# First stage of a transformer layer: modulation pair by pair, and transposes placed behind their copies

## The chip, the cores and the metric

The kernel runs on one core of a Trainium2 chip. The metric is the device time of one execution in microseconds (us). Three runs of the kernel before took 2655.70, 2655.83 and 2657.45 us, median 2655.83 us. The profiled execution took 2657.01 us; its span in the trace is 2655.3 us, so 1.71 us lie around the span.

## The reference

One layer of a hybrid backbone works on 256 latent tokens x and 256 context tokens ctx, both 2048 wide, all in fp32. What this case touches is its beginning:

```python
mod_x = (jax.nn.silu(c) @ w_mod[i] + b_mod[i]).reshape(bsz, 1, N_MOD, D_MODEL)
mod_c = (jax.nn.silu(c_ctx) @ w_mod[i] + b_mod[i]).reshape(1, 1, N_MOD, D_MODEL)

def _half_ffn(x, mod, k, g, w_gate, w_up, w_down):
    h = _modulate(_rms_norm(x, g), mod[:, :, 3 * k], mod[:, :, 3 * k + 1])
    f = (jax.nn.silu(h @ w_gate) * (h @ w_up)) @ w_down
    return x + 0.5 * mod[:, :, 3 * k + 2] * f
```

`_modulate(h, shift, scale)` is `h * (1 + scale) + shift`. The nine modulation vectors come from one matrix `w_mod` of 2048 x 18432, and parts 0 (shift) and 1 (scale) of it must be there before any row of h exists. The feed-forward has 5504 hidden columns. A token mixer, a second half feed-forward and a final norm follow; the change leaves them alone.

## The kernel before

All activations stand transposed: 16 tiles of 128 features by 512 tokens (256 latent, 256 context), taken two at a time as eight *K pairs*, kp 0 to 7. Each fp32 operand of a large matmul is split into a rounded high part and the rest, low: ScalarE casts the high part (L68), VectorE subtracts (L69), and one product becomes three matmuls (`mm3`, L116 to L118). The cast and the subtraction of a weight tile together are called its *split* below.

The first stage, the first 150 us, does three things at once. It transposes x and ctx and sums their squares for the norm. It computes parts 1 and 0 of the modulation on TensorE (L529): the weights arrive in loads of 512 KB, a *half* is the work on two loads, four halves fill one PSUM *bank* of 512 columns, VectorE copies the bank to SBUF (L373, the *copy*), TensorE transposes it in four pieces (L378, the *turn*), and VectorE reduces the pieces to columns, adds the bias and scales (L381, L386, L393). With `cnt == 2` the two parts have a bank each, and a bank serves two K pairs; the loads have rows of 2 KB. With `cnt == 1` one bank holds both parts of a single K pair, and the loads have rows of 1 KB. The turn and its columns let `first_h` run for the K pair: VectorE multiplies by the norm (L324), ScalarE applies scale and shift (L332, tiles hh), VectorE makes the low part (L337, tiles hl). Third, `first_cols` multiplies hh and hl of each K pair with the first 384 columns of the gate and up weights of the first feed-forward, 18 matmuls for gate and 18 for up per K pair; these add up in six PSUM banks over all eight K pairs.

The order is written by hand: the lists given to `weave` say behind which group of three matmuls ("place", twelve a K pair) each half, copy and turn stands. K pairs 0 and 1 have their modulation complete before the first such matmul. `run` hands out the load and the split of a task two tasks ahead, and `ahead` keeps three halves' loads in front. A scheduler may then move instructions on an engine, but TensorE's modulation matmuls and VectorE's copies are marked with `keep_in_program_order`. Each engine works through its own queue in order.

All these weights pass through one pool of seven buffers (`rp`, tiles raw), loaded from SyncE's queue in order; a load is issued when the last reader of its buffer is done. After this stage the kernel streams the rest of the weights with TensorE as the busy engine.

Of the kernel before, what the change touches and what calls it, by code (L numbers as in the profile page):

```python
# [34 lines left out]
def tile_block(ctx: ExitStack, tc: tile.TileContext, a, out: bass.AP):  # L35
# [280 lines left out]
    def modulated(kp, vs, R, G, S):  # L316

        st = {}
        a0, a1 = vs[0] * TX, (vs[-1] + 1) * TX

        def scale():
            for v in vs:
                st[v] = slot([P, 2, TX], n="xr")
                tt(st[v], xpair(kp, v), R(v).unsqueeze(1).broadcast_to([P, 2, TX]), op=ALU.mult)  # L324

        def affine():
            for i in range(2):
                k = 2 * kp + i
                t = st["t", i] = slot([P, a1 - a0], n="t")
                for dst in (hh[k][:, a0:a1], t):  # L330
                    for v in vs:
                        act(dst[:, v * TX - a0:(v + 1) * TX - a0], st[v][:, i, :], AF.Identity, scale=G(k, v), bias=S(k, v))  # L332

        def parts():
            for i in range(2):
                k = 2 * kp + i
                tt(hl[k][:, a0:a1], st["t", i], hh[k][:, a0:a1].bitcast(F32), op=ALU.subtract)  # L337

        return [(0.7, scale), (0.1, affine), (0.8 * len(vs), parts)]
# [56 lines left out]
    def column(part):  # L396
        return lambda k, v: MOD[part][:, k, v:v + 1]
# [153 lines left out]
    def first_h(kp):  # L551
        for _, f in modulated(kp, (0, 1), lambda v: R0["R"][:, v * TX:(v + 1) * TX], column(1), column(0)):
            f()

    m0, t0 = first_mods(0, 2)
    for load, _ in m0:
        if load:
            load()
    total, root, spread = [f for _, f in pieces]
    for f in (*[f for _, f in m0[:5]], total, small_turn, root, *[f for _, f in m0[5:7]], t0[0], spread,  # L560
              *[f for _, f in m0[7:]], *t0[1:], lambda: first_h(0)):
        f()

    between = {1: [lambda: first_h(1)]}
    later = []

    def place(at, f):
        between.setdefault(at, []).append(f)  # L570

    def weave(k0, cnt, at):
        steps, turns = first_mods(k0, cnt)
        for (load, f), x in zip(steps, at):
            if load:
                later.append(load)
            place(x, f)
            if load:
                place(x, ahead)
        place(at[len(steps)], lambda: [t() for t in turns])  # L580
        place(at[len(steps)], lambda: first_h(k0))
        if cnt == 2:
            place(12 * k0 + 1, lambda: first_h(k0 + 1))
# [2 lines left out]
        if later:  # L586
            later.pop(0)()

    weave(2, 2, [1, 3, 5, 7, 8, 9, 11, 13, 15, 16, 17])
    weave(4, 2, [19, 21, 24, 26, 27, 29, 32, 34, 37, 38, 39])  # L590
    weave(6, 1, [42, 46, 50, 54, 55, 56])
    weave(7, 1, [58, 62, 66, 70, 71, 73])

    g0 = []

# [106 lines left out]
    for ci, n in enumerate(chunks):  # L702
        m0 = m
# [707 lines left out]
    t0 = len(tasks) - 8  # L1411
# [108 lines left out]
```

## Time and profile before

| what | value |
|---|---|
| median of three runs | 2655.83 us |
| the profiled execution, its span | 2657.01 us, 2655.3 us |
| TensorE busy in the span | 2616.2 us (99%) |
| VectorE, ScalarE busy | 1617.7 us (61%), 979.6 us (37%) |
| first matmul of the feed-forward | at 49.03 us |

The page gives the busy time of each engine, then slices of the span, then the chain of work that ended last. Such shares are means over the whole span; the stretch of the change, from 18 to 150 us, is read in the timeline, instruction by instruction: which engine a wait of TensorE is put down to, and what that engine had been waiting for in its turn. A row of the timeline may stand for several instructions of one form (x8), and its bracket gives the idle time before it and what ended that.

### The profile page before, as it was taken

The page shows a single profiled execution, that of the slowest core. Times are in us where ns is not written, and L with a number is a line of the kernel's source. Part 1 is how long each engine was busy: PE and PEld are TensorE (multiplying, and loading weights), DVE is VectorE, ACT ScalarE, POOL GpSimd, SP SyncE. Part 2 cuts the span into 40 slices and gives each one's busy share as a digit, 9 for nine tenths or more (in the row PEclk, how much of TensorE's full clock was granted, in tenths as well). Part 3 has the DMA queues.
Part 4 walks back from the last instruction along what each step waited for, and adds up shares of the span by engine and source line. Part 5 has one row for each costly group of instructions (what it writes and reads, how often), then busy time and mean ns, then how long its engine had stood idle before and what let it go on. Part 6 is the DMA issues. An engine that isn't in the chain of part 4 may idle for free.

```text
span 2655.3 us, 31810 instructions
## 1 busy us (share of the span) xinstructions
PE 2616.2 (99%) x12309; PEld 2132.3 (80%) x12309; DVE 1617.7 (61%) x2167; ACT 979.6 (37%) x1326; POOL 56.2 (2%) x84
## 2 busy tenths in 40 slices
PE   6999999999999999999999999999999999999998
PEld 3577888888888888888889977778788888888896
DVE  3378987876555556556324855876654445455646
ACT  4342222212222222222223654765564443434344
POOL 2000000000000000000000000021010000000000
PEclk8999999999999999999999999999999999999999
DMA  9976766657665766766434543355666666666664
GB/s 314 317 240 201 224 211 203 195 172 211 203 194 164 217 189 207 220 190 205 119 102 132 175 131 88 111 173 164 199 199 189 192 189 194 188 195 186 196 179 139
DMA packets 333547, 499.06 MB, mean 188 GB/s; under 512 B 18835, under 2 KB 169683, under 8 KB 333395
## 3 DMA queue, kind: packets, MB, share of 16 engines
q1 hardware_dynamic: 331059, 491.21, 60.0%
q0 software_dynamic: 2336, 5.81, 0.9%
q8 instruction: 96, 1.57, 0.2%
q14 instruction: 56, 0.46, 0.0%
HBM read 492.77 MB, written 2.10 MB: 186 GB/s over the span
## 4 chain that ended last, share of the span: by engine, by line
PE 95%; DMA 2%; DVE 1%; ACT 1%; issue 0%; SPq 0%; ACTq 0%; DVEq 0%
PE gu L116 25%; PE gu L117 25%; PE gu L118 25%; PE dn L116 5%; PE dn L117 5%; PE dn L118 5%; PE mi L529 1%; DMA raw<-in_w_mod_dram 1%; PE dn L982 0%; DVE cy L903 0%; PE mi L411 0%; PE mi L1356 0%; PE mi L1052 0%; PE mi L1081 0%; ACT hi L68 0%
## 5 line engine op out<-in xcount | busy, mean ns | idle before, releaser
L69 DVE TENSOR_TENSOR lo<-raw,hi 128x1024 fp32r<-128x1024 f32 (+1 forms) x634 | 759.9, 1199 | 777.8 <-ACT hi L68 777.0
L68 ACT CAST hi<-raw 128x1024 fp32r<-128x1024 f32 (+1 forms) x634 | 650.1, 1026 | 1446.0 <-PE gu L117 755.5
L116 PE MATMUL gu<-hh,hi 128*128 128x512 f32 x1504 | 590.0, 393 | 1.9 <-ACT hh L332 1.6
L118 PE MATMUL gu<-hh,lo 128*128 128x512 f32 x1504 | 587.2, 390 | 0.0
L117 PE MATMUL gu<-hl,hi 128*128 128x512 f32 x1504 | 587.1, 390 | 0.0
L459 DVE SCALAR_TENSOR_TENSOR macc<-raw,sc,macc 128x512 f32<-128x512 f32 x600 | 424.5, 746 | 4.9
L116 PEld LDWEIGHTS gu<-hh,hi 128*128 128x128 f32 x1504 | 283.0, 188 | 75.5 <-issue 7.2
L116 PE MATMUL gu<-hi,hh 128*128 128x512 f32 (+1 forms) x864 | 336.3, 390 | 0.0
L117 PE MATMUL gu<-lo,hh 128*128 128x512 f32 (+1 forms) x864 | 334.3, 387 | 0.0
L118 PE MATMUL gu<-hi,hl 128*128 128x512 f32 (+1 forms) x864 | 333.6, 386 | 0.0
L117 PEld LDWEIGHTS gu<-hl,hi 128*128 128x128 f32 x1504 | 282.9, 188 | 61.2 <-issue 4.3
L118 PEld LDWEIGHTS gu<-hh,lo 128*128 128x128 f32 x1504 | 282.6, 188 | 61.3 <-issue 2.2
L116 PEld LDWEIGHTS gu<-hi,hh 128*128 128x128 f32 x864 | 162.3, 188 | 32.0 <-issue 1.4
L117 PEld LDWEIGHTS gu<-lo,hh 128*128 128x128 f32 x864 | 162.3, 188 | 31.8 <-issue 1.4
L118 PEld LDWEIGHTS gu<-hi,hl 128*128 128x128 f32 x864 | 162.2, 188 | 31.8 <-issue 0.7
L116 PE MATMUL gu<-ah,hi 128*128 128x512 f32 (+1 forms) x408 | 145.6, 357 | 0.0
L116 PE MATMUL dn<-ah,hi 128*128 128x512 f32 (+1 forms) x408 | 145.4, 356 | 0.0
L118 PE MATMUL dn<-ah,lo 128*128 128x512 f32 (+1 forms) x408 | 145.4, 356 | 0.0
L117 PE MATMUL dn<-al,hi 128*128 128x512 f32 (+1 forms) x408 | 145.2, 356 | 0.0
L117 PE MATMUL gu<-al,hi 128*128 128x512 f32 (+1 forms) x408 | 145.2, 356 | 0.0
L118 PE MATMUL gu<-ah,lo 128*128 128x512 f32 (+1 forms) x408 | 145.1, 356 | 0.0
L116 PEld LDWEIGHTS dn<-ah,hi 128*128 128x128 f32 x408 | 77.1, 189 | 12.6 <-ACT hi L68 0.8
(309 smaller groups left out, 2549.4 us busy)
## 6 DMA issues: line engine op xcount, KB each, us to landing
raw<-in_w_mod_dram SPq DMA_DIRECT2D x288, 512.0 KB, 4.7
raw<-in_ffn_w_down_dram SPq DMA_DIRECT2D x172, 512.0 KB, 3.9
raw<-in_ffn_w_gate_dram SPq DMA_DIRECT2D x160, 512.0 KB, 4.4
raw<-in_ffn_w_up_dram SPq DMA_DIRECT2D x160, 512.0 KB, 4.2
raw<-in_w_in_dram SPq DMA_DIRECT2D x72, 512.0 KB, 3.7
raw<-in_w_out_dram SPq DMA_DIRECT2D x32, 512.0 KB, 3.8
raw<-in_ffn_w_gate_dram SPq DMA_DIRECT2D x16, 384.0 KB, 4.0
raw<-in_ffn_w_up_dram SPq DMA_DIRECT2D x16, 384.0 KB, 3.4
```

Of the source, the lines that this page charges most:

```text
L68: a = nc.scalar.copy(hi, src)
L69: b = nc.vector.tensor_tensor(lo, src, hi.bitcast(F32), op=ALU.subtract)
L116: nc.tensor.matmul(ps, lhsT=wh, rhs=xh, start=first, stop=False)
L117: nc.tensor.matmul(ps, lhsT=wh, rhs=xl, start=False, stop=False)
L118: nc.tensor.matmul(ps, lhsT=wl, rhs=xh, start=False, stop=last)
L459: tc.keep_in_program_order(stt(acc[v], w[:, i, :], s, acc[v], op0=ALU.mult, op1=ALU.add))
L529: tc.keep_in_program_order(nc.tensor.matmul(o[32 * g:32 * g + 32, :], lhsT=sc[:, j, :], rhs=src, start=(j == first[g]), stop=(j == last[g])))
```

## The change

The first bank of modulation serves K pair 0 alone (`cnt == 1`: four halves in place of eight). K pair 1 has a bank of its own, woven into the matmuls of K pair 0. The places of all later halves, copies and turns are new; a turn is now listed two to three places behind its copy, where before it was one or two.

```diff
-    m0, t0 = first_mods(0, 2)
+    m0, t0 = first_mods(0, 1)
...
-    for f in (*[f for _, f in m0[:5]], total, small_turn, root, *[f for _, f in m0[5:7]], t0[0], spread,
-              *[f for _, f in m0[7:]], *t0[1:], lambda: first_h(0)):
+    for f in (*[f for _, f in m0[:2]], total, small_turn, root, m0[2][1], spread, m0[3][1], m0[4][1], *t0, lambda: first_h(0)):
         f()
...
-    between = {1: [lambda: first_h(1)]}
+    between = {}
...
-    weave(2, 2, [1, 3, 5, 7, 8, 9, 11, 13, 15, 16, 17])
+    weave(1, 1, [1, 3, 5, 7, 8, 10])
+    weave(2, 2, [9, 11, 12, 13, 14, 15, 16, 17, 18, 19, 22])
...
```

The lists for K pairs 4 and 5, 6, and 7 change in the same manner. In each list the entry behind every fourth half is the copy of the bank, and the last one the turn. How this stands on the engines is shown at three places. First VectorE at the start, around the copy of the last bank that `first_h(0)` needs, m_455 before and m_427 after; r and dg are the norm's factor, xr the first step of h, and lo_ the splits of gate and up weights. Before:

```order
L253 TENSOR_SCALAR r_419<-dn_403 128x4
L255 RECIPROCAL r_419<-r_419 128x4
L279 TENSOR_TENSOR dg_423<-ident,r_419 128x512
L381 TENSOR_REDUCE mod_311<-mi_434 128x4 x2
L386 TENSOR_TENSOR mod_311<-mod_311,vt 128x4 x2
L393 SCALAR_TENSOR_TENSOR mod_311<-mod_311,vt 128x8
L373 COPY m_455<-mi_425 128x512
L324 TENSOR_TENSOR xr_467<-xt_150,R_445 128x512
```

After:

```order
L255 RECIPROCAL r_401<-r_401 128x4
L279 TENSOR_TENSOR dg_405<-ident,r_401 128x512
L69 TENSOR_TENSOR lo_477<-raw_474,hi_476 128x768
L69 TENSOR_TENSOR lo_483<-raw_480,hi_482 128x768
L69 TENSOR_TENSOR lo_489<-raw_486,hi_488 128x768
L373 COPY m_427<-mi_368 128x512
L324 TENSOR_TENSOR xr_439<-xt_150,R_417 128x512
```

Behind dg, the three splits of the gate weights of K pairs 0 and 1 and the up weights of K pair 0 now stand ahead of the copy. Second, VectorE at the end of K pair 1; mi_625 (before) and mi_682 (after) are the second bank of K pairs 2 and 3, raw_648 and raw_646 the gate weights of K pair 2, raw_713 its up weights, and hl_329 the first low part of K pair 2. Before:

```order
L393 SCALAR_TENSOR_TENSOR mod_311<-mod_311,vt 128x8
L69 TENSOR_TENSOR lo_651<-raw_648,hi_650 128x768
L373 COPY m_685<-mi_625 128x512
L324 TENSOR_TENSOR xr_709<-xt_152,R_445 128x512
L324 TENSOR_TENSOR xr_711<-xc_160,R_445 128x512
L381 TENSOR_REDUCE mod_310<-mi_699 128x4 x2
L386 TENSOR_TENSOR mod_310<-mod_310,vt 128x4 x2
```

After:

```order
L69 TENSOR_TENSOR lo_649<-raw_646,hi_648 128x768
L373 COPY m_677<-mi_597 128x512
L381 TENSOR_REDUCE mod_311<-mi_744 128x4 x2
L386 TENSOR_TENSOR mod_311<-mod_311,vt 128x4 x2
L393 SCALAR_TENSOR_TENSOR mod_311<-mod_311,vt 128x8
L69 TENSOR_TENSOR lo_716<-raw_713,hi_715 128x768
L373 COPY m_733<-mi_682 128x512
L324 TENSOR_TENSOR xr_763<-xt_152,R_417 128x512
L324 TENSOR_TENSOR xr_765<-xc_160,R_417 128x512
L381 TENSOR_REDUCE mod_310<-mi_753 128x4 x2
L386 TENSOR_TENSOR mod_310<-mod_310,vt 128x4 x2
L337 TENSOR_TENSOR hl_329<-t_767,hh_328 128x512
```

The copy of that bank, m_685 before and m_733 now, has the split of the gate weights in front of it before, and those of the gate and of the up weights now. Third, TensorE at the same place; mi_699 and mi_753 are the turn of that bank, hh_328 is the first tile of K pair 2. Before:

```order
L118 MATMUL dn_525<-hh_326,lo_600 128x512
L529 MATMUL mi_625<-raw_632,sc 32x512 x2
L529 MATMUL mi_625<-raw_630,sc 32x512 x2
L378 MATMUL mi_699<-ident,m_685 128x128 x4
L529 MATMUL mi_737<-raw_646,sc 32x512 x2
L529 MATMUL mi_737<-raw_644,sc 32x512 x2
L529 MATMUL mi_737<-raw_666,sc 32x512 x2
L529 MATMUL mi_737<-raw_664,sc 32x512 x2
L116 MATMUL gu_520<-hh_328,hi_650 128x512
```

After:

```order
L117 MATMUL dn_497<-hl_327,hi_567 128x512
L118 MATMUL dn_497<-hh_326,lo_568 128x512
L529 MATMUL mi_682<-raw_689,sc 32x512 x2
L529 MATMUL mi_682<-raw_687,sc 32x512 x2
L378 MATMUL mi_753<-ident,m_733 128x128 x4
L116 MATMUL gu_492<-hh_328,hi_648 128x512
L116 MATMUL gu_493<-hh_328,hi_648 128x512
L116 MATMUL gu_494<-hh_328,hi_648 128x512
L116 MATMUL gu_495<-hh_328,hi_715 128x512
```

Before, two halves of the next bank stand between that turn and the first matmul of K pair 2, and now none; the turn stands right behind the bank's last half in both.

## Rows read from the trace of the kernel before

**Rows 1.** The page of the kernel before: span, busy time, chain by engine.

```profile
span 2655.3 us, 31810 instructions
PE 2616.2 (99%) x12309; PEld 2132.3 (80%) x12309; DVE 1617.7 (61%) x2167; ACT 979.6 (37%) x1326; POOL 56.2 (2%) x84
...
PE 95%; DMA 2%; DVE 1%; ACT 1%; issue 0%; SPq 0%; ACTq 0%; DVEq 0%
```

**Rows 2.** Windows (busy us of each engine, TensorE's granted clock, DMA share, GB/s).

```profile
50.00:60.00 10.00, 10.00 (x48) 5.49 (x46) 4.84 (x7) 6.81 (x13) 0.00 (x0) 0.81 0.75 260
...
150.00:160.00 10.00, 10.00 (x46) 8.29 (x45) 4.88 (x5) 5.70 (x7) 0.00 (x0) 1.00 0.57 161
```

**Rows 3.** Timeline (start us, us, engine line op, idle before and releaser), TensorE, 24 to 33.

```profile
24.63 1.93 PE L529 MATMUL mi<-raw,sc 128*32 128x512 f32 x8 [1.57 <-DMA raw<-in_w_mod_dram]
...
32.66 1.37 PE L529 MATMUL mi<-raw,sc 128*32 128x512 f32 x8
```

**Rows 4.** Windows with loads of 2 KB rows and of 1 KB rows.

```profile
26.00:30.00 4.00, 2.54 (x16) 0.25 (x15) 0.69 (x1) 2.62 (x4) 1.38 (x2) 0.50 1.05 387
...
118.00:122.00 4.00, 4.00 (x32) 2.65 (x36) 2.52 (x4) 3.22 (x7) 0.00 (x0) 1.00 1.05 359
...
122.00:126.00 4.00, 4.00 (x30) 2.84 (x24) 0.99 (x2) 1.77 (x3) 0.00 (x0) 1.00 1.09 357
```

**Rows 5.** Timeline, from the last bank's copy to the first matmuls.

```profile
45.59 0.69 DVE L373 COPY m<-mi 128x512 f32<-128x512 f32 x1 [7.40 <-PE mi L529]
...
49.03 2.07 PE L116 MATMUL gu<-hh,hi 128*128 128x512 f32 x4 [1.59 <-ACT hh L332]
...
53.59 1.15 PE L529 MATMUL mi<-raw,sc 128*32 128x512 f32 x8
```

**Rows 6.** Timeline, TensorE, K pair 1 and start of K pair 2.

```profile
64.34 0.39 PE L116 MATMUL gu<-hh,hi 128*128 128x512 f32 x1
...
66.50 1.06 PE L529 MATMUL mi<-raw,sc 128*32 128x512 f32 x8
...
76.72 1.06 PE L529 MATMUL mi<-raw,sc 128*32 128x512 f32 x8
...
79.80 0.66 PE L378 MATMUL mi<-ident,m 128*128 128x128 f32 x4 [2.02 <-DVE m L373]
...
83.29 1.52 PE L116 MATMUL gu<-hh,hi 128*128 128x512 f32 x3
```

**Rows 7.** Timeline, weight loads, their splits, and copies, 61 to 111.

```profile
61.07 0.42 SPq L62 DMA_DIRECT2D raw<-in_ffn_w_up_dram  x1
...
67.89 0.83 ACT L68 CAST hi<-raw 128x768 fp32r<-128x768 f32 x1 [10.06 <-DMA raw<-in_ffn_w_up_dram]
...
79.06 0.68 DVE L373 COPY m<-mi 128x512 f32<-128x512 f32 x1
...
79.17 0.37 SPq L62 DMA_DIRECT2D raw<-in_ffn_w_up_dram  x1
...
109.92 0.96 DVE L69 TENSOR_TENSOR lo<-raw,hi 128x768 fp32r<-128x768 f32 x1 [5.79 <-ACT hi L68]
...
110.79 0.68 DVE L373 COPY m<-mi 128x512 f32<-128x512 f32 x1
```

**Rows 8.** Timeline, TensorE, its later waits and what follows them.

```profile
88.96 1.06 PE L529 MATMUL mi<-raw,sc 128*32 128x512 f32 x8 [0.86 <-DMA raw<-in_w_mod_dram]
...
111.53 0.87 PE L378 MATMUL mi<-ident,m 128*128 128x128 f32 x4 [2.27 <-DVE m L373]
...
112.33 3.35 PE L529 MATMUL mi<-raw,sc 128*32 128x256 f32 x32
...
131.38 0.66 PE L378 MATMUL mi<-ident,m 128*128 128x128 f32 x4 [1.13 <-DVE m L373]
...
131.97 1.93 PE L529 MATMUL mi<-raw,sc 128*32 128x256 f32 x32
```

**Rows 9.** DMA issues of the page (count, KB each, median us to landing).

```profile
raw<-in_ffn_w_up_dram SPq DMA_DIRECT2D x16, 384.0 KB, 3.4
```

More of the change, by code (lines that the diff above doesn't have):

```diff
@@ L587, in ahead @@
             later.pop(0)()
-    weave(2, 2, [1, 3, 5, 7, 8, 9, 11, 13, 15, 16, 17])
-    weave(4, 2, [19, 21, 24, 26, 27, 29, 32, 34, 37, 38, 39])
-    weave(6, 1, [42, 46, 50, 54, 55, 56])
-    weave(7, 1, [58, 62, 66, 70, 71, 73])
+    weave(1, 1, [1, 3, 5, 7, 8, 10])
+    weave(2, 2, [9, 11, 12, 13, 14, 15, 16, 17, 18, 19, 22])
+    weave(4, 2, [24, 26, 28, 30, 31, 32, 34, 36, 38, 39, 42])
+    weave(6, 1, [44, 47, 50, 53, 54, 57])
+    weave(7, 1, [59, 62, 65, 68, 69, 72])
     g0 = []
```

## The prediction

> **What bounds the kernel now.** I read the page first: TensorE is busy 99% of the span and holds 95% of the chain that ended last [rows 1]. What an edit of 150 us can be worth must therefore lie in the TensorE time that is lost there, and whatever TensorE gains or loses before 150 us reaches the end, because after its last wait, before 131.38 us [rows 8], it is busy for all of a window, as from 150 to 160 us [rows 2]. Second, the timeline of the start: until 49.03 us TensorE runs halves as their loads come [rows 3, 5]. Third, the windows: from 22 us the 16 DMA engines are full, at 387 GB/s, with a dip to 260 GB/s between 50 and 60 us [rows 2, 4]. Fourth, the timeline from 60 to 132 us: TensorE waits again at 79.80, 88.96, 111.53 and 131.38 us, three times for the copy of a finished bank [rows 6, 8]. The reader is to see in rows 7 what held the copy before 111.53 us: VectorE's queue had the split of gate weights in front of it, and that split waited for its own load.
>
> The sum goes by positions: where TensorE starts K pairs 0, 1 and 2, and how much modulation it has done by then. Every number is against the profiled execution, 2657.01 us, which is 1.2 us above the median of the runs; the difference found is then put on the median, 2655.83 us.
>
> **Start of K pair 0.** Before, the halves of the first bank start at 24.63 and 32.66 us and at two times between them, 2.68 us each, so a 512 KB load takes 1.34 us [rows 3]. After, four halves do instead of eight, with rows of 1 KB. Such loads ran between 118 and 126 us at 357 to 359 GB/s where 2 KB rows had 387 [rows 4]: 1.46 us each, so the eighth lands near 33.4 us. Behind it come three weight loads of 393 KB, about 1.03 us each: 36.5 us. All three splits now stand ahead of the copy in VectorE's queue, so the copy waits for the last: cast 0.83 and subtraction 0.96 us [rows 7] make 38.3 us. From the start of the copy to the first matmul took 45.59 to 49.03 us, 3.44 us [rows 5]: 41.7 us. With the two small operations more that a shared bank has, and the last half standing behind the spread of the norm, I take 42.5 us: 6.5 us early. Bounds: 38.4 us, if the copy followed the last half (33.4, some 1.5 for the half, and 3.44), and 44.5 us, if the norm's chain is late by one half.
>
> The Trainium skill, "DMA: Bandwidth & Descriptors", section Specifications, gives 512 B as the smallest transfer for the full rate, so by it 1 KB rows cost nothing, and eight loads would land 1.0 us earlier. Rows 4 show them 8% slower in this kernel, and the measurement decides; the sum above does not use the rule.
>
> **K pair 0 to K pair 1.** Before, 36 matmuls and four halves took 49.03 to 64.34 us, 15.3 us [rows 5, 6]. After there are six halves, 1.06 us each [rows 6]: 17.4 us, so TensorE reaches the turn at 59.9 us. The first copy of the new bank stands behind the split of the up weights of K pair 1, as the bank's copy is listed behind the start of that task. That load is the 24th (the 32nd before), and its buffer comes free when the third half of K pair 0 is done: ten matmuls at the low clock, 4.6 us (49.03 to 53.59 us) [rows 5], eleven at 0.24 us (nine between 64.34 and 66.50 us) [rows 6] and three halves, near 53 us. From issue to cast it took 61.07 to 67.89 us before, 6.8 us [rows 7], and the median of such loads is 3.4 us [rows 9]. I take 58 us, between them, and with the split 59.9 us. Then 3.44 us: K pair 1 starts at 63.4 us, against 64.34. The early start is nearly gone, and two halves are owed: before, four halves of the next banks were done here, after two. That is 2.1 us, so TensorE is 1.2 us behind. What hid this chain before: `first_h` of K pair 1 needed no bank of its own.
>
> **K pair 1 to K pair 2.** 36 matmuls at 0.24 us, six halves, and two turns of 0.35 us make 15.7 us; after a wait of over 3 us the clock starts low, which cost 1.4 us at 112.33 us (32 short matmuls in 3.35 us where 131.97 us shows 1.93) [rows 8]. So the bank's last half ends at 80.5 us. Its copy now stands behind the split of K pair 2's up weights, the 42nd load, five behind the bank's own last. Before, only the gate weights stood in front, three loads behind the bank's last, and the copy came 1.3 us after the half: half from 76.72, copy at 79.06 us [rows 6, 7]. Price of the new order: the buffers are all full while TensorE waits for K pair 1, so the next eleven loads start when its first half frees buffers, eight matmuls and one half at the low clock (1.93 us for a half at granted clock 0.50, the lower of its two levels [rows 3, 4]), some 5.6 us after 63.4: 69 us. The first lands 3.4 us later, nine follow at 1.34 and the up weights at 1.03: 85.5 us. Split 1.8 and chain 3.44 us: K pair 2 starts near 90.7 us. Lower bound: no load is late, 80.5 plus 3.44, 83.9 us. Between them: only this load's own issue counts, behind the fifth half, 77.5 plus 3.4, 1.8 and 3.44, 86.1 us. I take 90 us, near the count of loads, since DMA was the full resource around there. Before it was 83.29 us, with two halves of the next bank already done in the meantime; after, none stands between the turn and K pair 2. So 6.7 plus 2.1: 8.8 us behind.
>
> **The rest of the stage.** Given back: the wait of 1.13 us at 131.38 us, since that turn now stands nine matmuls later; against it the later K pairs again have two more halves each to fit beside loads that start late. The wait of 2.27 us at 111.53 us keeps its cause, a split in front of the copy, and the list's three places change nothing in that; it may shrink by up to 2 us, since TensorE comes later and the loads do not. I count 0.8 us back. Sum: 8.0 us slower, 2665.0 us in a profile, 2663.8 us as a median. All other moves (places of halves, names of buffers) change no amount of work: as many matmuls, copies, splits and bytes as before; I cost them at nothing, covered by the seven buffers, and at 1 to 2 us either way if that cover is short.
>
> **Rivals.**
> - *Slower by more, 2669 us.* The loads issued behind K pair 2 are late too, so the missing cover repeats: 8.8 us behind and a new wait of about 4 us at K pair 3 or 4. For it: a stall fills all seven buffers and stops the loads, as the dip between 50 and 60 us shows [rows 2]. Against it: before has one such dip at the start and recovers. 15%.
> - *No change, 2656 us.* The up weights of K pair 2 land in time: 83.9 us for K pair 2, 0.6 plus 2.1 us behind, with 2 to 3 us given back at 88.96, 111.53 and 131.38 us. For it: DMA idles less in the first 60 us than before. Against it: the order on VectorE forces the wait as soon as that load is later than 80 us, and before it was issued at 79.17 us, only two loads further on [rows 7]. 22%.
> - *Faster, 2649 us.* The 6.5 us of the start stay, because splits are ready ahead of all copies and the new chain at K pair 1 costs nothing; that needs the copies to come out at least 3 us before TensorE reaches the turns. For it: the lists say two to three places. Against it: a place is three matmuls, 0.7 us, so three places are 2.1 us, less than the 3.44 us of the chain, and in TensorE's order the turn of K pair 2 has not moved from the bank's last half. 8%.
> - *The forecast, 2664 us.* 55%; its own range is 2659 to 2668 us.
>
> That the change does not do what it says is part of these: the turns are listed later, but the copies are held by what stands in front of them on VectorE.
>
> **How the numbers follow.** Runs of this kernel tell a change from none at about 0.2%, 5.3 us, so slower means above 2661.1 us. The forecast gives slower in four of five cases (0.44), the first rival 0.15, the no-change case 0.05, and the rest goes to same: slower 0.64. Faster is below 2650.5 us: 0.08 from the third rival and 0.02 from the second: 0.10. Same: 0.26. The range of eight in ten goes from 2654 us (K pair 2 at the lower bound) to 2672 us (a full repeat of the stall).
>
> **What would show it.** Right: the first matmul (L116) near 42 us; a wait of TensorE of 4 us in two pieces around 60 us, put down to the copy (L373) and then to hh (L332); a wait of 6 us or more before the turn near 87 us, with a split (L69) that ends just before the copy; K pair 2 starting after 88 us. Wrong: the copy of that bank starting within 2 us of its last half, or the first matmul of K pair 2 before 84 us. If K pair 2 is late but the end is not, loads in the later K pairs gave the time back, and my 0.8 us was too little.

## The result and the profile after

The changed kernel takes 2672.91 us (median of six runs, 2671.77 to 2674.36), the kernel before 2655.93 us (six runs, 2655.32 to 2657.45): a ratio of 1.0062, 95% interval 1.0051 to 1.0073. It is slower by 17.0 us. The forecast was 2664 us with a range of 2654 to 2672: the direction came out, the loss is twice the size, and the median lies 0.9 us past the range.

The page of the changed kernel, which answers to [rows 1]:

```profile
span 2672.7 us, 31939 instructions
...
PE 2622.6 (98%) x12373; PEld 2139.2 (80%) x12373; DVE 1617.9 (61%) x2168; ACT 979.1 (37%) x1326; POOL 56.1 (2%) x84
...
PE 93%; DMA 3%; DVE 2%; ACT 2%; issue 0%; SPq 0%; ACTq 0%; DVEq 0%
```

TensorE holds 93% of the chain that ended last, not 95%; DMA, VectorE and ScalarE have taken the rest. Where the time went is seen at one landmark that both kernels have: the first activation of the feed-forward (L615), which runs when the first stage is over. Timeline of ScalarE, before:

```profile
152.54 0.60 ACT L615 ACTIVATE sg<-gu 128x512 f32<-128x512 f32 x1 [0.55 <-PE gu L118]
```

After:

```profile
170.18 0.60 ACT L615 ACTIVATE sg<-gu 128x512 f32<-128x512 f32 x1
```

It comes 17.6 us later, and from it to the end of the span is 2502.8 us before and 2502.5 us after. The whole loss lies in the first stage. Not all of it is waiting: TensorE's busy time is 6.4 us more than before (2622.6 against 2616.2 us) for the same columns, and its granted clock was lower there (0.78 from 66.97 to 97.12 us, K pair 1 to K pair 2, where the kernel before had 0.94 from 64.34 to 83.29). TensorE's timeline, after (start, duration, work, idle time before and what ended it), answers to [rows 5, 6]:

```profile
42.06 1.11 PE L378 MATMUL mi<-ident,m 128*128 128x128 f32 x4 [0.81 <-DVE m L373]
44.95 2.08 PE L116 MATMUL gu<-hh,hi 128*128 128x512 f32 x4 [1.78 <-ACT hh L332]
...
64.17 0.66 PE L378 MATMUL mi<-ident,m 128*128 128x128 f32 x4 [1.43 <-DVE m L373]
66.97 2.07 PE L116 MATMUL gu<-hh,hi 128*128 128x512 f32 x4 [2.14 <-ACT hh L332]
...
94.42 1.12 PE L378 MATMUL mi<-ident,m 128*128 128x128 f32 x4 [9.32 <-DVE m L373]
97.12 2.07 PE L116 MATMUL gu<-hh,hi 128*128 128x512 f32 x4 [1.59 <-ACT hh L332]
```

K pairs 0, 1 and 2 start at 44.95, 66.97 and 97.12 us, against 49.03, 64.34 and 83.29. With 1.06 us for each half that is still owed (four at K pair 0, two at the others) the kernel stands 0.2 us behind, then 4.8, then 16 us, and 17.6 us at the end of the stage. In this execution pair by pair gains nothing even at the start: 4.1 us early, four halves owed.

What held the two copies, in the timelines of SyncE, ScalarE and VectorE after (compare [rows 7]):

```profile
55.73 0.42 SPq L62 DMA_DIRECT2D raw<-in_ffn_w_up_dram  x1
...
61.69 0.83 ACT L68 CAST hi<-raw 128x768 fp32r<-128x768 f32 x1 [13.84 <-DMA raw<-in_ffn_w_up_dram]
...
62.56 0.96 DVE L69 TENSOR_TENSOR lo<-raw,hi 128x768 fp32r<-128x768 f32 x1 [13.98 <-ACT hi L68]
...
63.43 0.68 DVE L373 COPY m<-mi 128x512 f32<-128x512 f32 x1
...
71.62 11.07 SPq L62 DMA_DIRECT2D raw<-in_w_mod_dram  x10
...
82.78 0.42 SPq L62 DMA_DIRECT2D raw<-in_ffn_w_up_dram  x1
...
85.12 1.64 SPq L62 DMA_DIRECT2D raw<-in_w_mod_dram  x2
...
91.94 0.83 ACT L68 CAST hi<-raw 128x768 fp32r<-128x768 f32 x1 [19.63 <-DMA raw<-in_ffn_w_up_dram]
92.80 0.96 DVE L69 TENSOR_TENSOR lo<-raw,hi 128x768 fp32r<-128x768 f32 x1 [8.72 <-ACT hi L68]
93.68 0.68 DVE L373 COPY m<-mi 128x512 f32<-128x512 f32 x1
```

The reader is to see twice the same chain of up weights, cast, subtraction, copy. The second bank was complete at 85.1 us (its last half starts at 84.03), and its copy ran at 93.68, right behind a split whose weights had been issued at 82.78. VectorE did nothing at all in the 8.72 us before that split, with the copy's bank complete. The Trainium skill, "Perfetto Trace Analysis", section "Tensor Engine Instruction (MATMUL, LD_WEIGHTS)", calls VectorE's queue strictly first in, first out; this trace agrees, with those 8.7 us.

Windows after (busy us of each engine, clock, DMA share, GB/s) show what the wait does to the loads:

```profile
38.00:40.00 2.00, 2.00 (x10) 0.40 (x12) 1.85 (x3) 1.01 (x2) 0.00 (x0) 0.50 0.42 91
...
48.00:50.00 2.00, 2.00 (x12) 1.00 (x15) 0.58 (x1) 0.00 (x0) 0.00 (x0) 0.55 0.10 35
50.00:52.00 2.00, 2.00 (x23) 1.00 (x14) 0.00 (x0) 0.00 (x0) 0.00 (x0) 1.00 0.17 40
...
70.00:72.00 2.00, 2.00 (x12) 0.48 (x11) 0.59 (x1) 0.53 (x1) 0.00 (x0) 0.93 0.03 12
...
90.00:100.00 10.00, 4.00 (x11) 3.02 (x12) 3.90 (x9) 4.86 (x10) 0.00 (x0) 0.50 0.26 84
```

While TensorE waits, and until its next half, no half frees a buffer, and the loads stop: near 50, 71 and 95 us. Near 39 us it is the late splits that hold the buffers (SyncE's queue waits 3.8 us for L69 there). In the kernel before the emptiest window of 10 us between 20 and 110 us is the one from 50 to 60 us, with 260 GB/s [rows 2]. What SyncE's queue waited for between 60 and 110 us, after (us in total, times, longest):

```profile
SPq L62 <- PE mi L529: 26.6, 12, 7.8
```

It waited most for halves (L529) to be done with their buffers. By 80 us 17.7 MB had come since 20 us, against 21.0 MB before (the sum of six windows of 10 us; so are all such figures below).

### The profile page after: what moved, and what is told of

It is laid out like the page before. It is cut to its first block, busy times and chain, and to the rows that moved or that the text cites. A ratio compares the mean times of both kernels' runs of the same rounds, so it can differ in the third digit from the quotient of the medians.

```text
span 2672.7 us, 31939 instructions
## 1 busy us (share of the span) xinstructions
PE 2622.6 (98%) x12373; PEld 2139.2 (80%) x12373; DVE 1617.9 (61%) x2168; ACT 979.1 (37%) x1326; POOL 56.1 (2%) x84
## 4 chain that ended last, share of the span: by engine, by line
PE 93%; DMA 3%; DVE 2%; ACT 2%; issue 0%; SPq 0%; ACTq 0%; DVEq 0%
PE gu L116 25%; PE gu L117 25%; PE gu L118 25%; PE dn L116 5%; PE dn L117 5%; PE dn L118 5%; DMA raw<-in_ffn_w_up_dram 1%; DMA raw<-in_w_mod_dram 1%; PE mi L529 1%; DMA xin<-in_ctx_dram 0%; PE dn L982 0%; DVE cy L903 0%; PE mi L411 0%; PE mi L1356 0%; ACT hi L68 0%
## 5 line engine op out<-in xcount | busy, mean ns | idle before, releaser
L69 DVE TENSOR_TENSOR lo<-raw,hi 128x1024 fp32r<-128x1024 f32 (+1 forms) x634 | 759.8, 1199 | 795.8 <-ACT hi L68 786.6
L118 PEld LDWEIGHTS gu<-hi,hl 128*128 128x128 f32 x864 | 162.2, 188 | 31.8 <-issue 0.7
```

The source lines that it names most:

```text
L69: b = nc.vector.tensor_tensor(lo, src, hi.bitcast(F32), op=ALU.subtract)
L118: nc.tensor.matmul(ps, lhsT=wl, rhs=xh, start=False, stop=last)
```

## The experiments

Each row of the table compares a kernel with the kernel before, run beside it. MB is what was loaded between 20 and 80 us, and the end of the stage is the start of that first activation, both in the profiled execution of that kernel; this one execution may lie up to 4 us from the median. The column of MB does not order the kernels by itself: "every split late" in the kernel before has 20.3 MB and loses nothing, "two splits, cover at the start" has 20.5 MB and is 4 us slower. In the diffs below, lines that are left out are marked with three dots.

| kernel | median us | ratio to before, 95% interval | MB | stage ends |
|---|---|---|---|---|
| after | 2672.9 | 1.0062 [1.0051, 1.0073] | 17.7 | 170.2 |
| turns one place behind | 2673.9 | 1.0063 [1.0051, 1.0076] | 17.9 | 167.1 |
| second copy free | 2664.8 | 1.0033 [1.0021, 1.0046] | 18.8 | 160.5 |
| both copies free, by two splits | 2661.8 | 1.0022 [1.0013, 1.0030] | 19.3 | 157.4 |
| both copies free, by closer halves | 2662.3 | 1.0024 [1.0015, 1.0033] | 19.5 | 156.4 |
| every split late | 2662.4 | 1.0024 [1.0015, 1.0032] | 19.8 | 155.5 |
| two splits, start reordered | 2664.1 | 1.0030 [1.0018, 1.0041] | 19.0 | 159.8 |
| two splits, cover at K pair 2 | 2660.9 | 1.0018 [1.0009, 1.0026] | 19.2 | 154.1 |
| two splits, cover at the start | 2660.4 | 1.0014 [1.0005, 1.0024] | 20.5 | 153.0 |
| after, eight buffers | 2667.2 | 1.0047 [1.0033, 1.0061] | 19.1 | 162.2 |
| two splits, eight buffers | 2660.5 | 1.0014 [1.0005, 1.0023] | 19.4 | 155.1 |
| two splits, cover at the start, eight buffers | 2657.0 | 1.0002 [0.9993, 1.0011] | 20.6 | 152.3 |
| before, turns later | 2655.3 | 0.9998 [0.9989, 1.0007] | 20.9 | 152.0 |
| before, second copy late | 2663.6 | 1.0027 [1.0015, 1.0038] | 20.6 | 159.3 |
| before, every split late | 2655.7 | 1.0003 [0.9994, 1.0012] | 20.3 | 154.5 |
| before, rows of 1 KB at the start | 2657.7 | 1.0005 [0.9997, 1.0014] | 19.9 | 153.4 |
| before, eight buffers | 2653.6 | 0.9991 [0.9982, 0.9999] | 21.5 | 149.8 |
| the same, one split late | 2650.3 | 0.9979 [0.9970, 0.9988] | 21.9 | 144.6 |

### Free the copies

In the first run the loads and all places stay, and only two splits move.

```diff
+    LATE = {1: 9, 2: 20}
...
-        add(loaded([P, 2, N0 * P], krows(w, 2 * kp, 2, 0, N0 * P)), mm)
+        shape, src = [P, 2, N0 * P], krows(w, 2 * kp, 2, 0, N0 * P)
+        if n and kp in LATE:
...
+            place(LATE[kp], lambda: st.update(s=split(st["w"], shape)))
+            add(fetch, lambda d: mm(d["s"]))
+        else:
+            add(loaded(shape, src), mm)
```

`LATE` gives the place of the split for the up weights (`n` is 1) of K pairs 1 and 2, and `fetch` is the load alone.

> The changed kernel, with the split of the up weights of K pairs 1 and 2 listed behind the copy of the bank (places 9 and 20); the loads, their order and all places of halves, copies and turns stay. Theory (VectorE's queue holds the copy behind that split, and its stall repeats because the loads stop meanwhile): K pair 1 starts at about 65 us (66.97 after), the copy before K pair 2 within 2 us of its bank's last half, K pair 2 at 86 to 89 us (97.12 after), the dip of the DMA engines between 90 and 100 us goes, and the time is 2660 to 2666 us, against 2672.9 after and 2655.9 before. Rival, too few loads in time: the copies come early, but TensorE waits as long for the same up weights at their own matmuls: 2669 to 2673 us. Rival, an extra chain of copy, turn and h at K pair 1 is the cost in itself: unchanged, 2671 to 2674 us.

TensorE and VectorE with the two splits late, from K pair 1 to K pair 2:

```profile
63.45 1.19 PE L116 MATMUL gu<-hh,hi 128*128 128x512 f32 x4 [0.83 <-ACT hh L332]
...
81.03 0.69 DVE L373 COPY m<-mi 128x512 f32<-128x512 f32 x1 [4.67 <-PE mi L529]
...
81.77 0.66 PE L378 MATMUL mi<-ident,m 128*128 128x128 f32 x4 [0.91 <-DVE m L373]
...
84.38 0.97 PE L116 MATMUL gu<-hh,hi 128*128 128x512 f32 x3 [1.95 <-ACT hh L332]
```

and its window:

```profile
90.00:100.00 10.00, 10.00 (x53) 5.38 (x53) 2.39 (x4) 3.91 (x7) 0.00 (x0) 1.00 1.01 357
```

The copy now waits for its own bank (PE L529), K pair 2 starts 12.7 us earlier (1.6 us earlier than expected), the stop between 90 and 100 us is gone, and 11.1 of the 17.0 us come back. This changes the order of VectorE and ScalarE and no amount of work: that the copies stood behind those splits is shown as the cause of two thirds of the loss.

Two more ways to the same end. The first frees the second copy alone, the other both, by halves that come closer together:

```diff
-weave(2, 2, [9, 11, 12, 13, 14, 15, 16, 17, 18, 19, 22])
+weave(2, 2, [9, 10, 11, 12, 13, 14, 15, 16, 17, 17, 22])
```

> The changed kernel with the halves of K pairs 2 and 3 at places 9 to 17 and the second copy at 17, the bank of K pair 1 as it is: only the second copy is ahead of its split. Theory: the 1.4 us wait before the turn of K pair 1 stays, the 9.3 us one before that of K pair 2 goes: 2663 to 2667 us, that is 6 to 9 of the 11 us. Rival, the delay at K pair 1 is what makes the loads of K pair 2 late: 2668 us or more.

Its two turns, TensorE:

```profile
64.73 0.66 PE L378 MATMUL mi<-ident,m 128*128 128x128 f32 x4 [2.37 <-DVE m L373]
...
83.58 0.66 PE L378 MATMUL mi<-ident,m 128*128 128x128 f32 x4 [0.91 <-DVE m L373]
```

The wait at K pair 1 stays (2.37 us) and the other shrinks from 9.32 to 0.91 us, as expected: some 8 of the 11 us belong to the second copy. The 3 us that are left for the first are no more than the two intervals leave open.

```diff
-weave(1, 1, [1, 3, 5, 7, 8, 10])
+weave(1, 1, [1, 2, 3, 5, 5, 10])
```

This edit with the one above it:

> The changed kernel, with the halves of the bank of K pair 1 at places 1, 2, 3 and 5 and its copy at 5, and those of K pairs 2 and 3 at places 9 to 17 without a gap and the second copy at 17; turns stay at 10 and 22. Both copies then stand ahead of the splits of the up weights on VectorE, though the halves come closer together. Theory: K pair 2 starts at 87 to 91 us with no dip of the DMA engines from 90 to 100 us, 2661 to 2668 us. Rival, too few loads in time: the closer halves wait for their loads by as much as the copies gain: 2669 to 2674 us.

It took 2662.3 us, and K pair 2 started at 83.41 us, earlier than expected: the same gain, with the splits where they were.

Last, the same order put into the kernel before, where the start keeps its pairs:

```diff
-weave(2, 2, [1, 3, 5, 7, 8, 9, 11, 13, 15, 16, 17])
+weave(2, 2, [1, 3, 5, 7, 8, 9, 11, 13, 15, 19, 22])
```

> The kernel before, with the copy of the second bank of K pairs 2 and 3 at place 19 instead of 16 and both turns at 22 instead of 17; the pairing of the start stays. On VectorE the copy then has the split of K pair 2's up weights in front of it. Two halves of the next bank stand ahead of the turns on TensorE, and they free four buffers while it waits. Theory: a wait before the turns near 85 us that the copy and that split end, K pair 2 at 86 to 90 us (83.29 before), and 2657 to 2664 us, less than the changed kernel because the loads go on. Rival, only the pairing costs: 2654 to 2657 us, and no wait over 2.5 us before the turns.

```profile
85.65 0.96 DVE L69 TENSOR_TENSOR lo<-raw,hi 128x768 fp32r<-128x768 f32 x1 [6.47 <-ACT hi L68]
86.53 0.68 DVE L373 COPY m<-mi 128x512 f32<-128x512 f32 x1
...
87.27 1.11 PE L378 MATMUL mi<-ident,m 128*128 128x128 f32 x4 [5.79 <-DVE m L373]
```

These rows of VectorE and TensorE show split, copy and turn in a row, and a wait of 5.79 us where there were 2.02 [rows 6]. K pair 2 starts at 91.49 us, 1.5 us past what was expected, and the time is within the 2657 to 2664 us. Without any of the pair-by-pair start the kernel loses 7.5 us (2663.64 against 2656.19). The stop of the loads comes here too, at 90 to 100 us (90 GB/s), after the 80 us that the column of MB counts.

### Not the distance of the turns

In the changed kernel with turns one place behind their copies:

```diff
-weave(1, 1, [1, 3, 5, 7, 8, 10])
+weave(1, 1, [1, 3, 5, 7, 8, 9])
...
```

The last entries of the other lists become 20, 40, 55 and 70.

> The changed kernel, with each turn one place behind its copy instead of two or three (places 9, 20, 40, 55 and 70); halves and copies stay. Theory: the copies stand where they stood, so K pair 2 still starts near 97 us, and the later turns wait up to 1 us more each: 2671 to 2676 us. Rival, the later turns are what costs: 2656 to 2666 us.

And in the kernel before, with the turns three places behind:

```diff
-weave(2, 2, [1, 3, 5, 7, 8, 9, 11, 13, 15, 16, 17])
+weave(2, 2, [1, 3, 5, 7, 8, 9, 11, 13, 15, 16, 19])
...
```

The last entries of the other lists become 41, 58 and 74.

> The kernel before with each turn listed three places behind its copy (19, 41, 58 and 74 instead of 17, 39, 56 and 73), and nothing else changed: the second part of the change alone. On VectorE the copy of each bank keeps what stood in front of it. Theory: copies come when they came, the waits of 2.02, 2.27 and 1.13 us before turns shrink by up to 2 us together, against it less cover behind the turn: 2653 to 2657 us, no change that can be told. Rival, the later turns make the first matmuls of the next K pair late: 2659 us or more.

Neither can be told from its base: 2673.9 and 2655.3 us. In the changed kernel K pair 2 starts at 95.43 us behind a wait of 7.96 us that the copy ends; in the kernel before the turn at 79.14 us waits 1.92 us for its copy. So listing the turns later, the second part of the change, makes no difference that these runs can tell.

### Too few buffers, and where

```diff
-NSLOT = 70
+NSLOT = 68
...
-rp = ctx.enter_context(tc.tile_pool(name="rp", bufs=7))
+rp = ctx.enter_context(tc.tile_pool(name="rp", bufs=8))
```

> The changed kernel with eight raw buffers instead of seven (two slots less in the pool of the other tiles); all orders stay. Rival under test, the number of buffers is the cause: K pair 2 starts before 90 us and the time is 2658 to 2665 us. Theory: one load more fits while TensorE waits, so the up weights of K pair 2 land 1 to 2 us earlier and the copy still waits for their split: K pair 2 at 94 to 96 us, 2669 to 2672 us.

```profile
88.23 0.96 DVE L69 TENSOR_TENSOR lo<-raw,hi 128x768 fp32r<-128x768 f32 x1 [6.98 <-ACT hi L68]
89.11 0.68 DVE L373 COPY m<-mi 128x512 f32<-128x512 f32 x1
...
92.54 2.07 PE L116 MATMUL gu<-hh,hi 128*128 128x512 f32 x4 [1.59 <-ACT hh L332]
```

Both expectations missed. The copy still stands behind the split, as the theory says, but K pair 2 comes 4.6 us earlier and the time falls by 5.7 us, more than the 1.34 us of one load. That the buffer counts at each of the stops is a reading; no run shows it stop by stop. The same buffer in the kernel before:

> The kernel before with eight raw buffers: what a buffer is worth where no copy stands behind a late split by much. Theory: the dip of the loads between 50 and 60 us shrinks by one load, 1.34 us, and the waits for copies whose splits are late shrink by as much: 2652 to 2655 us. Rival, loads are not what bounds the stage: 2655 to 2657 us.

2653.6 us, as the theory had it: a buffer is worth 2.7 us in the kernel before, and 5.7 us in the changed kernel. With the two splits late:

> The changed kernel with the two late splits and eight raw buffers. With the copies free, what is left of the loss (some 6 us) is put down to loads: 19.3 MB had come between 20 and 80 us, 21.0 MB in the kernel before, a difference of 4.3 us at 387 GB/s. Theory: an eighth buffer lets one load more come while TensorE waits at the start: 2658 to 2660 us. Rival, the loss is in the chains of copy, turn and h alone: 2661 to 2663 us.

2660.5 us lies between the two expectations and cannot be told from 2661.8; the eighth buffer alone does not close the gap.

The stop near 40 to 50 us comes because nothing frees a buffer while TensorE waits for the norm and the first h. The next run gives it something to do there:

```diff
+    m1, t1 = first_mods(1, 1)
...
-for f in (..., m0[4][1], *t0, lambda: first_h(0)):
+for f in (..., m0[4][1], t0[0], m1[0][1], m1[1][1], *t0[1:], lambda: first_h(0)):
...
-    weave(1, 1, [1, 3, 5, 7, 8, 10])
+    weave(1, 1, [3, 6, 8, 10])
```

> The changed kernel with the two late splits, and two halves of the bank of K pair 1 run at the start, between the turn of the first bank and the first matmul, so that four buffers come free some 8 us earlier; the other halves of that bank at places 3 and 6. Theory (the rest of the loss is that all seven buffers are full from 36 us until the first halves among the matmuls): K pair 0 starts near 46 us, 1.5 us later than with the late splits alone, but two halves further, the dip of the loads between 40 and 50 us (235 GB/s) goes up to 300 GB/s or more, and 2656 to 2659 us. Rival, loads before 50 us are worth nothing: 2661 to 2664 us.

K pair 0 starts at 44.14 us, not near 46: the two halves fit into the wait for the first h. The window from 40 to 50 us goes from 235 to 289 GB/s, and in the profiled execution, one of the fastest of its runs, the stage ends at 153.0 us. The median, 2660.4 us, stays above what was expected and cannot be told from 2661.8; the runs spread from 2656.5 to 2664.7 us. Both together:

> The changed kernel with the two late splits, two halves of K pair 1's bank run at the start, and eight raw buffers: all that the runs name against the stop of the loads. Theory: nothing of the loss is left but the narrower rows: 2655 to 2658 us, level with the kernel before or within 2 us of it, though not level with the kernel before with eight buffers (2653.6). Rival, a chain of its own at K pair 1 costs: 2659 to 2662 us.

2657.0 us is level with the kernel before (1.0002, 0.9993 to 1.0011), as the theory had it. But the eighth buffer helps the kernel before as well: with eight buffers on both sides, 3.4 us remain (2657.0 against 2653.6), and without the cover at the start it was 6.9 (2660.5 against 2653.6). So the cover gives back about half of what is left with eight buffers, and the rest is not explained by these runs.

### What does not help, and the narrow rows

Three edits on top of the late splits: the last half and its copy ahead of the norm's spread; two halves of K pairs 4 and 5 around the last turn before K pair 2; and all splits from K pair 1 on six places ahead of their first matmul (in the changed kernel and in the kernel before).

```diff
...
-root, m0[2][1], spread, m0[3][1], m0[4][1], *t0
+root, m0[2][1], m0[3][1], m0[4][1], spread, *t0
...
```

> The changed kernel with the two late splits, and at the start the last half of the first bank and its copy listed ahead of the norm's spread. Theory: the last half starts as its load is there, near 36 us instead of 39 us, the first matmul of K pair 0 at 42 to 43.5 us instead of 44.6 us, and that carries over: 2659 to 2661 us, against 2661.8. Rival, the norm is what is late in any order, as its root and spread run at the lower clock: no gain, 2661 to 2663 us.

```diff
-weave(4, 2, [24, 26, 28, 30, 31, 32, 34, 36, 38, 39, 42])
+weave(4, 2, [21, 22, 25, 28, 30, 32, 34, 36, 38, 39, 42])
```

> The changed kernel with the two late splits, and the first two halves of K pairs 4 and 5 at places 21 and 22, so that two halves of the next bank stand around the last turn before K pair 2, as in the kernel before. Theory (loads bound this stretch: 374 and 380 GB/s from 60 to 80 us): the halves wait for their loads instead, 2660 to 2663 us, no better than 2661.8. Rival, the lost cover is the rest of the loss: 2657 to 2659 us.

```diff
+    EARLY = 6
...
+        at = 12 * kp + 6 * n - EARLY
+        if at > 0:
...
+            place(at, lambda: st.update(s=split(st["w"], shape)))
...
```

> The changed kernel with the same edit: every split from K pair 1 on six places ahead of its first matmul. Theory: as the run with the two splits listed late (2661.8 us), less the waits at 114.81 and 135.56 us there, some 2.5 us: 2658 to 2661 us. Rival, buffers held longer: 2663 to 2668 us. If pair by pair were worth the whole 4 us of its earlier start, it would come out at 2652 us or less.

> The kernel before, with the split of every gate and up weight from K pair 1 on listed six places ahead of its first matmul instead of up to twelve; loads, halves, copies and turns stay. Theory (a split whose load is late holds the copy behind it): the waits of 2.02 us at 79.80 and 2.27 us at 111.53 us shrink to about 1 us each, which is what a copy behind its bank's last half costs, and 2652 to 2655 us. Rival, the raw weights sit in their buffers longer and the loads behind them come later: 2657 to 2662 us, with new waits of TensorE for loads of w_mod.

The first: the norm's spread then runs at 40.27 us, the first matmul of K pair 0 at 46.02 us, and nothing is gained, as the rival had it, though its median of 2664.1 us lies 1.1 us above the rival's range too. The second: 2660.9 us, as expected from loads that bound the stretch; one of its halves waits 1.82 us for its load at 82.24 us. The third missed its 2658 to 2661 us by 1.4, and the fourth found no gain where 1 to 4 us were expected. In TensorE's timeline of the kernel before with all splits late:

```profile
80.16 0.66 PE L378 MATMUL mi<-ident,m 128*128 128x128 f32 x4 [0.91 <-DVE m L373]
...
86.43 0.80 PE L116 MATMUL gu<-hh,hi 128*128 128x512 f32 x1 [3.63 <-ACT hi L68]
```

The wait for the copy shrinks to 0.91 us and a new one of 3.63 us for the up weights themselves takes its place. So a split is worth listing late only where a copy stands behind it.

The rows of the loads by themselves, in the kernel before (first two banks):

```diff
-w.append(raw([P, 2, 512], wmod[:, j0 + 2 * x:j0 + 2 * x + 2, n0:n0 + 512]))
+w.append(raw([P, 4, 256], wmod[:, r:r + 4, c:c + 256]))
...
```

A half is then sixteen matmuls of 256 columns in place of eight of 512, as in the changed kernel.

> The kernel before, with the sixteen loads of the first two banks (K pairs 0 and 1) in rows of 1 KB instead of 2 KB, as the changed kernel has them: as many bytes, the same order. A load of such rows took 1.48 us, one of 2 KB rows 1.34 us. Theory: sixteen times 0.14, 2.2 us, as the loads are what the start waits for: first matmul of K pair 0 at 51 us (49.03 before) and 2657 to 2659 us. Rival, the narrower rows are hidden: 2655 to 2657 us.

The window from 30 to 36 us has 351 GB/s against 386, and K pair 0 starts at 50.15 us, 1.1 us later instead of the 2 expected. The ratio, 1.0005 (0.9997 to 1.0014), does not tell 1.4 us from nothing. The Trainium skill, "DMA: Bandwidth & Descriptors", section Specifications, has the full rate from 512 B on; the rate measured here, 351 against 386 GB/s, is 9% lower with rows of 1 KB than with rows of 2 KB, and the measurement decides.

### A version that beats both

In the kernel before with eight buffers one copy still waits behind a split, that of the gate weights of K pair 4 (VectorE and TensorE):

```profile
107.94 0.96 DVE L69 TENSOR_TENSOR lo<-raw,hi 128x768 fp32r<-128x768 f32 x1 [6.12 <-ACT hi L68]
108.81 0.68 DVE L373 COPY m<-mi 128x512 f32<-128x512 f32 x1
...
109.55 0.66 PE L378 MATMUL mi<-ident,m 128*128 128x128 f32 x4 [3.21 <-DVE m L373]
```

```diff
+    LATE = {4: 41}
...
+        if n == 0 and kp in LATE:
...
```

Here `n == 0` picks the gate weights.

> The kernel before with eight raw buffers and one split more listed late: that of the gate weights of K pair 4, at place 41, behind the copy of the second bank of K pairs 4 and 5. In the run with eight buffers alone TensorE waits 3.21 us at 109.55 us for that copy. Theory: the wait shrinks to about 0.85 us, what a copy behind its bank's last half costs, the stage ends some 2 us earlier, and 2650.5 to 2652.5 us against 2653.6. Rival, the wait turns into one for the same weights at their own matmuls: 2653 to 2655 us.

```profile
101.14 0.69 DVE L373 COPY m<-mi 128x512 f32<-128x512 f32 x1 [0.93 <-PE mi L529]
...
102.93 0.60 PE L378 MATMUL mi<-ident,m 128*128 128x128 f32 x4
...
108.79 0.50 PE L116 MATMUL gu<-hh,hi 128*128 128x512 f32 x1 [0.73 <-ACT hi L68]
```

The copy follows its half, the turn waits for nothing, and the late weights cost 0.73 us. 2650.3 us: 0.9979 of the kernel before (0.9970 to 0.9988), a little better than expected, and 22.6 us below the changed kernel. Each against the kernel before run beside it, the eighth buffer alone gained 2.7 us and buffer and split together 5.3; the two intervals just overlap, so the size of the split's share is not sure. So the kernel before, too, lost time to a copy behind a late split.

## Why the prediction missed the size

The mechanism, copies that stand behind splits with late loads, was right. Two steps of the sum failed: the wait behind the up weights of K pair 2, sized at 6.1 us, and the cover by the seven buffers, put at nothing. Place by place:

- **Start of K pair 0: right in direction, 2.45 us short.** 42.5 us was given, 44.95 measured. The sum had the copy wait for the three splits and the splits for their loads. The step that failed is the norm's chain, which was taken as if nothing changed there: it held both. On ScalarE the casts stand behind the norm's root (L254) and follow it without a gap; the splits were done at 39.85 us, not 38.3; and the copy waited 1.46 us more, for the last half, which stands behind the norm's spread (L283). TensorE, ScalarE and VectorE, after:

```profile
32.22 3.57 PE L272 MATMUL dn<-ones,sq 128*128 128x1 f32 x16
...
37.30 2.08 PE L283 MATMUL dn<-dg,ones 128*128 128x512 f32 x2 [1.51 <-DVE dg L279]
39.31 1.94 PE L529 MATMUL mi<-raw,sc 128*32 128x256 f32 x16
...
36.03 0.20 ACT L254 ACTIVATE r<-r 128x4 f32<-128x4 f32 x1 [7.28 <-DVE r L253]
36.14 2.28 ACT L68 CAST hi<-raw 128x768 fp32r<-128x768 f32 x3
...
37.16 2.69 DVE L69 TENSOR_TENSOR lo<-raw,hi 128x768 fp32r<-128x768 f32 x3
41.31 0.69 DVE L373 COPY m<-mi 128x512 f32<-128x512 f32 x1 [1.46 <-PE mi L529]
```

  The first two lines in the kernel before:

```profile
33.96 1.95 PE L272 MATMUL dn<-ones,sq 128*128 128x1 f32 x16
...
37.41 1.12 PE L283 MATMUL dn<-dg,ones 128*128 128x512 f32 x2
```

  A half took 1.07 us there, so the three together took 3.45 us less. The granted clock was 0.50, the lower of the two levels, in the window from 30 to 40 us, where the kernel before had 0.83. Why it did not rise here the runs do not show: in both kernels TensorE had run halves with waits between them until then. The order of the start does not decide it, as the kernel before with eight buffers has 0.50 in that window and 3.58 us for L272. The upper bound, 44.5 us, was passed by 0.45; over the six profiled executions with seven buffers and this order of the start, K pair 0 started between 43.17 and 45.55 us.
- **K pair 0 to K pair 1: the mechanism right, 1.1 us short.** The copy behind the split of the up weights, and the wait in two pieces (1.43 and 2.14 us), are as predicted. The load was issued at 55.73 us instead of 53, which is the start's delay, and came to its cast 6.0 us later instead of 5.
- **K pair 1 to K pair 2: the mechanism right, mis-sized by 3.6 us.** K pair 2 was put at 90 us, later than before by 6.7, and started at 97.12. Half of the 7.1 us between is what K pair 1 was late (66.97, not 63.4); the rest is the time that the eleven loads took. From the issue of the first at 71.62 us to the cast at 91.94 us it was 20.3 us, where the sum has 16.5. The windows from 72 to 92 us moved 6.7 MB; the eleven loads are 5.6 MB, and the two issued behind them at 85.12 us bring it to 6.7, so these ran in between: 2.7 us at 1.34 us each. Of the 256 packets of the up weights 240 were through before 89 us, and the last 16 came between 89 and 92 us, while those two loads ran; why they came so late the runs do not show. By its own terms the sum priced the late up weights of K pair 2 at 6.1 us (90 us against 83.9 with no load late); freeing that copy alone gave back 8.1 us, and freeing both 11.1. The upper end of the range allowed a wait of 4 us further on, not a larger one here.
- **The rest of the stage: the wrong sign.** 0.8 us were given back in the sum; 1.7 us more were lost in the profile (15.9 at K pair 2, 17.6 at the end). The first rival forecast a stop of the loads behind K pair 2, and they did stop at 90 to 100 us, but that is not where the 1.7 us come from: with the two splits late, where the loads go on (357 GB/s), the stretch from K pair 2 to the end of the stage takes 73.0 us, as long as here (73.1); before it took 69.25 us, and two halves that are owed are 2.1 of the difference. What makes the rest stays open.
- **"I cost them at nothing, covered by the seven buffers."** This was the other step that failed. With no load late the sum leaves 1.9 us (2.7 at K pair 2 less 0.8); the kernel with both copies free is 5.6 us slower than the kernel before. Its loads are behind from the start: 1.7 MB less by 80 us, 4.3 us at 387 GB/s, though the table shows that this is not time lost one for one. With eight buffers, halves that run while TensorE waits at the start bring the distance to the kernel before with eight buffers from 6.9 to 3.4 us, so missing cover at the start is a part of it. What makes the other 3 us, the narrow rows, the extra chain at K pair 1 or something else, stays open.
- **The rivals.** That the up weights land in time (no change) and that the early start is kept (faster) both fell with the rows of the copy at 93.68 us. For the first, the forecast counted on fewer gaps of the loads in the first 60 us; there were more, 11.9 MB from 20 to 60 us against 14.1 before.

## What to carry to other kernels

In front of every short instruction that another engine waits for, look at what stands in its own queue, and ask for the load behind that: if the load is issued later than the last one the short instruction itself needs, the wait is decided by the load. Then ask what frees buffers while that engine waits; where nothing does, the loads stop, and what they were to bring comes later. Here, moving halves from the start, where loads set the pace, into later matmuls gained nothing, as it also took away what freed the buffers.

## What the runs showed of the hardware

- The last packets of a load can come well behind the others: of the up weights issued at 82.78 us, 240 of 256 packets were through before 89 us and 16 came between 89 and 92 us, while two loads issued 2.3 us later ran. In the kernel before, of the up weights issued at 61.07 us, 240 were through before 65.8 us and 16 came in the 2.2 us after that. (They are the packets between 512 B and 2 KB in the DMA view of these stretches: 318 less 78 and 49 less 33 in the changed kernel, 302 less 62 and 33 less 17 before; the other weights there come in packets of 2 KB.)
- Loads with rows of 2 KB ran at 387 and 390 GB/s between 26 and 34 us in the kernel before; with rows of 1 KB they ran at 357 to 359 GB/s between 118 and 126 us, and at 351 GB/s from 30 to 36 us in the kernel before with narrow rows.
- Sixteen matmuls of one column (L272) took 3.57 us in the changed kernel at granted clock 0.50, and 1.95 us in the kernel before, where the clock from 34 to 36 us was 1.00.
